# Differential attention: values as the stationary operand, column-tiled softmax sums, products in PSUM between groups, finalization on token tiles moved by transfers

## Chip, cores, metric

The kernel runs on the 8 cores of one Trainium2 chip. Each core takes half of one sequence of the batch (2048 of its 4096 tokens as queries, all 4096 as keys). The metric is device time of the slowest core in microseconds (us). A program on all 8 cores has a second, slower state in some executions (a die with a lower granted clock); only fast runs are compared here unless the text says otherwise.

Engines: PE is TensorE's matmul and PEld its weight load, DVE is VectorE, ACT is ScalarE, POOL is GpSimd, SP is SyncE, whose queue issues most transfers.

## The reference, cut to what matters

```python
h = rmsnorm(x); z = h @ w_in                    # q k v gate | B C h gate
s1 = q1 @ k1.T / sqrt(d) + bias                 # bias = -slope[h] * |t - s|, 4 heads, d = 64
s2 = q2 @ k2.T / sqrt(d) + bias
probs = softmax(s1) - lam * softmax(s2)
o = probs @ v                                   # v is 128 wide
o = rmsnorm(o) * subln_g * (1 - lambda_init) * silu(gate)
x = x + concat(o, conv_branch) @ w_out          # then a gated embedding and a final norm
```

The slopes are 1/4, 1/16, 1/64 and 1/256. Blocks so far from the diagonal that the exponential is zero are skipped, so head 0 has few tiles (10 or 13 a unit), head 1 has 19 to 31, and heads 2 and 3 have 35. A *unit* is one head and 512 queries; there are 16. A *tile* is 128 keys by up to 512 queries, for both score sets: a *full tile* has all 512.

## The kernel before

Attention works tile by tile, two tiles deep: score pair of tile i on PE, exponential on ACT, then PV of tile i-2 on PE. Keys above the diagonal (group B) and the rest (group AC) are accumulated apart, because the bias is split into a part per key (in the exponential's bias) and a part per query, which differs between the groups.

```python
# PV: the exponentials are stationary, the values (with a column of ones, so 129) move
for r in [j_*4 + b_ for j_ in range(2) for b_ in range(b0, b1)]:          # up to 8 matmuls
    PE.matmul(acc_region(r), lhsT=ET[e][:, j*512 + sb_*128 : ...+128], rhs=VA[:, kt, h, :], ...)
# group B's end: DVE copies three PSUM banks to SBUF times fB[query] (a query is a partition)
# group AC's end: DVE adds three PSUM banks to that; then the finalization:
DVE: reciprocal [128x8]; x neglam; 4 x scale; 4 x combine; square; reduce     # query on partitions
POOL: variance, pow(-1/2) [128x4], scale [128x512]
PE (12 tiles later): 4 transposes;  DVE: x subln x gate -> MIXA
```

Each engine runs its own program in order. `X.need(t)` puts a wait for event t into X's program; `pending` delays the emission of a piece of work by so many tiles. `barrier()` after the last unit separates attention from the output stage. Before it, PE has other work: the first output tile and 32 transposes.

Of the kernel before, what the change touches and what calls it, by code (L numbers as in the profile page):

```python
# [6 lines left out]
F32 = mybir.dt.float32  # L7
# [9 lines left out]
NH = 4  # L17
# [44 lines left out]
def build_program(debug=None):  # L62
# [25 lines left out]
    with es:  # L88
# [17 lines left out]
        VAF = sb("VA", [128, 32 * NH * 129], BF16)  # L106
# [29 lines left out]
        iotaF = sb("iotaF", [128, 4], F32)  # L136
        iotaB0 = sb("iotaB0", [128, 32], F32)
        iotaF0 = sb("iotaF0", [128, 2, 2], F32)
        biasA = sb("biasA", [128, NH, 16], F32)
        biasB = sb("biasB", [128, NH, 32], F32)  # L140
        fB = sb("fB", [128, NH, 8], F32)
        rs = [sb("rs%d" % i, [128, 8], F32) for i in range(2)]
        c2 = [sb("c2_%d" % i, [128, 4], F32) for i in range(2)]
        ssq = [sb("ssq%d" % i, [128, 4], F32) for i in range(2)]
        vsq = [sb("vsq%d" % i, [128, 4], F32) for i in range(2)]
        rsd = [sb("rsd%d" % i, [128, 4], F32) for i in range(2)]
# [35 lines left out]
        POOL.eng.memset(mx_all[:], 0.0)  # L182
        tk_pc = POOL.mark(POOL.eng.memset(VA[:, :, :, 128:129], 1.0))
# [3 lines left out]
        LC = {}  # L187

        def late_consts():
# [18 lines left out]
            POOL.eng.iota(iotaB0[:], pattern=[[128, 32]], base=-255, channel_multiplier=1, allow_small_or_imprecise_dtypes=True)  # L208
            POOL.eng.iota(iotaF0[:], pattern=[[0, 2], [256, 2]], base=-255, channel_multiplier=2, allow_small_or_imprecise_dtypes=True)
            t_io = POOL.mark(POOL.eng.iota(iotaF[:], pattern=[[256, 4]], base=-511, channel_multiplier=2,  # L210
# [3 lines left out]
            for h in range(NH):  # L214
                src_f = iotaF0[:].rearrange("p a b -> p (a b)") if h == 0 else iotaF[:]
                for j_ in range(2):
                    LC["t_f"] = ACT.mark(ACT.eng.activation(out=fB[:, h, 4 * j_:4 * j_ + 4], in_=src_f, func=AF.Exp, scale=SLOPES[h]))

# [23 lines left out]
        with pes:  # L242
# [154 lines left out]
            def v_tile(buf, tl, rglob, ready_tk):  # L397
                s = psp_next()
                PE.need(psP_free[s], w_ready[buf], ready_tk)
                ins = None  # L400
                for c in range(8):
                    ins = PE.eng.matmul(psP[s][:], lhsT=HT[:, c, tl * 128:(tl + 1) * 128], rhs=WB[buf][:, c, :],  # L402
                                        start=(c == 0), stop=(c == 7))
                tk = PE.mark(ins)
                flush_deferred()
                DVE.need(tk, tk_pc)
                psP_free[s] = DVE.mark(DVE.eng.tensor_copy(out=VA[:, rglob, :, 0:128],
                                                           in_=psP[s][:].rearrange("p (h d) -> p h d", h=NH)))
# [165 lines left out]
        OACC = [cv.take([128, 8, 129], F32) for _ in range(2)]  # L574
        OT = [cv.take([128, 4, 128], F32) for _ in range(2)]
        ON = [cv.take([128, 4, 128], F32) for _ in range(2)]
# [23 lines left out]
        rc2 = RawCarver(VAF[:], 32 * NH * 129 * 2)  # L600
# [52 lines left out]
        with pes:  # L653
            psS = [es.enter_context(nc.psum_tensor("psS%d" % i, [128, 1024], F32)) for i in range(2)]
            psBig = es.enter_context(nc.psum_tensor("psBig", [128, 2048], F32))
            psA = [psBig[:, b_ * 512:(b_ + 1) * 512] for b_ in range(3)]
            psO = psBig[:, 1536:2048]

            def acc_region(r):
                return psA[r // 3][:, (r % 3) * 129:(r % 3) * 129 + 129]  # L660
# [11 lines left out]
            for h in range(NH):  # L672
                for qc in range(4):
                    unit = h * 4 + qc
                    rel = range(-4 * qc, 32 - 4 * qc)
                    up = [(n, live_range(h, n, 0, min(n, 4))) for n in rel if n > 0]
                    past = [(n, live_range(h, n, 0, 4)) for n in rel if n < 0]
                    past = [e_ for e_ in past if e_[1]]
                    diag = [(n, (n, min(4, live_range(h, n, 0, 4)[1]))) for n in range(4)]
                    ac = past[:2]  # L680
                    rest = past[2:]
                    for d_ in diag:
                        ac.append(d_)
                        ac += rest[:1]
                        rest = rest[1:]
                    groups = [("B", up), ("AC", ac + rest)]
                    groups = [(g, [e_ for e_ in els if e_[1]]) for g, els in groups]
                    for gi, (g, els) in enumerate(groups):
                        last_mm = {}
                        for ki, (n, (b0, b1)) in enumerate(els):  # L690
                            for r in [j_ * 4 + b_ for j_ in range(2) for b_ in range(b0, b1)]:
                                last_mm[r // 3] = (ki, r)
                        for ki, (n, (b0, b1)) in enumerate(els):
                            tiles.append(dict(h=h, qc=qc, unit=unit, g=g, n=n, kt=4 * qc + n, b0=b0, b1=b1, ki=ki, last_mm=last_mm,
                                              first=(ki == 0), last=(ki == len(els) - 1),
                                              unit_last=(gi == len(groups) - 1 and ki == len(els) - 1)))
# [6 lines left out]
            acc_done = {}  # L703
            started = set()
            oacc_free = [None, None]
            ot_free = [None, None]
            on_free = [None, None]
            pso_free = [P1END["psM"]]
            pending = []
            unit_evac = {}  # L710
# [30 lines left out]
            def finalize_part1(unit, h, qc, tks):  # L741
                u = unit % 2
                DVE.need(tks, ot_free[u])
                t_ = DVE.mark(DVE.eng.reciprocal(out=rs[u][:], in_=OACC[u][:, :, 128]))
                DVE.need(t_, LC["tk_const"])
                t_c2 = DVE.mark(DVE.eng.tensor_scalar(out=c2[u][:], in0=rs[u][:, 4:8], scalar1=neglam[:], scalar2=None, op0=ALU.mult))
                DVE.need(t_c2)
                for sb_ in range(4):
                    t_ = DVE.mark(DVE.eng.tensor_scalar(out=OT[u][:, sb_, :], in0=OACC[u][:, 4 + sb_, 0:128],
                                                        scalar1=c2[u][:, sb_:sb_ + 1], scalar2=None, op0=ALU.mult))  # L750
                DVE.need(t_)
                for sb_ in range(4):
                    t_ = DVE.mark(DVE.eng.scalar_tensor_tensor(out=OT[u][:, sb_, :], in0=OACC[u][:, sb_, 0:128],
                                                               scalar=rs[u][:, sb_:sb_ + 1], in1=OT[u][:, sb_, :],
                                                               op0=ALU.mult, op1=ALU.add))
                oacc_free[u] = t_
                DVE.need(t_)
                DVE.need(on_free[u])
                t_ = DVE.mark(DVE.eng.tensor_tensor(out=ON[u][:], in0=OT[u][:], in1=OT[u][:], op=ALU.mult))
                DVE.need(t_)  # L760
                t_ = DVE.mark(DVE.eng.tensor_reduce(out=ssq[u][:], in_=ON[u][:], axis=AX.X, op=ALU.add))  # L761
                DVE.need(t_)
                POOL.need(t_)
                t_v = POOL.mark(POOL.eng.tensor_scalar(out=vsq[u][:], in0=ssq[u][:], scalar1=1.0 / 128.0, scalar2=EPS,  # L764
                                                       op0=ALU.mult, op1=ALU.add))
                POOL.need(t_v)
                t_p = POOL.mark(POOL.eng.tensor_tensor(out=rsd[u][:], in0=vsq[u][:], in1=mhalf[:].to_broadcast([128, 4]), op=ALU.pow))
                POOL.need(t_p, on_free[u])
                t_on = POOL.mark(POOL.eng.tensor_tensor(out=ON[u][:], in0=OT[u][:],
                                                        in1=rsd[u][:].unsqueeze(2).to_broadcast([128, 4, 128]), op=ALU.mult))  # L770
                ot_free[u] = t_on

                def part2():
                    PE.need(t_on, pso_free[0])
                    ins = None
                    for sb_ in range(4):
                        ins = PE.eng.transpose(out=psO[:, sb_ * 128:(sb_ + 1) * 128], in_=ON[u][:, sb_, :], identity=ident_f[:])  # L777
                    t_tr = PE.mark(ins)
                    on_free[u] = t_tr
                    DVE.need(t_tr)  # L780
                    t_m = DVE.mark(DVE.eng.scalar_tensor_tensor(out=MIXA[:, h, qc * 512:(qc + 1) * 512], in0=psO[:], scalar=sublns[:],  # L781
                                                                in1=SGA[:, h, qc * 512:(qc + 1) * 512], op0=ALU.mult, op1=ALU.mult))
                    pso_free[0] = t_m
# [310 lines left out]
```

## Time and profile before

| | before |
|---|---|
| median | 963.2 us (fast runs 961.1 to 963.3) |
| projections and convolution | to 366 us |
| attention, heads 0 and 1 | 149.5 us |
| attention, heads 2 and 3 | 279.7 us |
| hand-over (last PV to first output-stage addition) | 14.7 us |
| output stage | the rest |

The head of the page of the kernel before: span and the busy time of each engine, with its share.

```profile
span 961.9 us, 17031 instructions; the slowest of 8 cores (956.1 to 961.9 us)
...
PE 838.9 (87%) x6210; PEld 445.6 (46%) x6210; DVE 450.7 (47%) x814; ACT 584.3 (61%) x783; POOL 123.5 (13%) x155
```

Busy time by stretch, kernel before: rows are heads 0 and 1, heads 2 and 3, hand-over. After the busy times come the granted PE clock, the share of DMA and GB/s.

```profile
core 5: us, PE busy (x) PEld busy (x) DVE busy (x) ACT busy (x) POOL busy (x), PEclk, DMA share, GB/s
366.50:516.00 149.50, 126.41 (x1181) 74.60 (x1179) 69.03 (x174) 125.00 (x167) 20.61 (x27) 0.88 0.23 33
516.00:795.70 279.70, 255.02 (x2634) 154.15 (x2635) 70.29 (x183) 265.97 (x278) 17.91 (x24) 0.99 0.06 17
795.70:810.35 14.65, 9.75 (x52) 6.81 (x50) 5.93 (x17) 4.10 (x4) 2.24 (x3) 0.78 0.00 1
```

ACT is busy 266 of the 280 us of heads 2 and 3: that stretch is bound by the exponentials, and PE has room. Over the whole span PE has the largest share (87%), which says nothing of this stretch. The timeline of two full tiles of head 2 (start, length, engine, what):

```profile
599.74 7.15 ACT L737 ACTIVATE ARENA<-psS,biasB 128x1024 bf16<-128x1024 f32 x7
...
600.00 0.37 PE L718 MATMUL psS<-QT,KT 64*128 64x512 bf16 x1
...
600.00 0.39 PE L720 MATMUL psS<-QT,KT 64*128 64x512 bf16 x1
...
600.32 0.63 PE L805 MATMUL psBig<-VA,ARENA 128*128 128x129 bf16 x8
...
601.00 0.37 PE L718 MATMUL psS<-QT,KT 64*128 64x512 bf16 x1
```

A tile repeats every 1.007 us (600.00 to 601.00 and so on). ACT runs seven exponentials without a gap. PE is done at 600.95 and starts the next score pair when ACT frees the score buffer. The two score matmuls lie in the two row halves of the array and run together.

### The profile page before, as it was taken

How to read it: one execution, taken by the hardware profiler on the slowest of the kernel's cores; microseconds unless marked ns; L12 is line 12 of the kernel's file. 1: busy time of each engine (PE TensorE's matmuls, PEld its weight loads, DVE VectorE, ACT ScalarE, POOL GpSimd, SP SyncE). 2: the span in 40 equal slices, each digit the busy share in tenths (PEclk: the TensorE clock that was granted, in tenths of full speed). 3: DMA queues.
4: the chain of work that ended last, by engine and by line, in shares of the span. 5: the costliest groups of instructions: out<-in, count | busy, mean ns of one | idle time of the engine just before them, and what ended most of it. 6: DMA issues, size and time to landing. Idle time of an engine off the chain costs nothing.

```text
span 961.9 us, 17031 instructions; the slowest of 8 cores (956.1 to 961.9 us)
## 1 busy us (share of the span) xinstructions
PE 838.9 (87%) x6210; PEld 445.6 (46%) x6210; DVE 450.7 (47%) x814; ACT 584.3 (61%) x783; POOL 123.5 (13%) x155
## 2 busy tenths in 40 slices
PE   0688979999999996889889999899999897999993
PEld 0344434444444443445555555555555554444441
DVE  1577684343277667644432213312312313577775
ACT  2344554502211116779999999999999992455553
POOL 2221130011110002010000000000000001122222
PEclk9999999999999997888999999999999997999997
DMA  8763422055550006700000000000500000133332
GB/s 175 203 154 96 140 73 42 4 44 45 44 44 1 2 1 84 114 1 1 2 2 1 2 2 1 2 1 4 174 1 1 2 1 22 53 124 132 132 110 88
DMA packets 37920, 51.04 MB, mean 53 GB/s; under 512 B 18512, under 2 KB 29392, under 8 KB 37840
## 3 DMA queue, kind: packets, MB, share of 16 engines
q1 hardware_dynamic: 12336, 36.85, 12.0%
q0 software_dynamic: 25504, 13.11, 11.9%
q8 instruction: 52, 0.85, 0.4%
q14 instruction: 28, 0.23, 0.1%
HBM read 54.67 MB, written 8.39 MB: 66 GB/s over the span
## 4 chain that ended last, share of the span: by engine, by line
PE 61%; DVE 13%; ACT 12%; issue 8%; DMA 2%; POOL 2%; DVEq 0%; SPq 0%; ACTq 0%; POOLq 0%
PE psP L357 20%; PE psBig L805 16%; PE psS L718 11%; ACT ARENA L737 8%; PE psP L402 6%; DMA ARENA<-x 2%; PE psS L900 2%; PE psS L950 2%; POOL r L916 2%; DVE VA L961 2%; DVE VA L965 1%; DVE KT L904 1%; ACT SGA L911 1%; DVE psS L728 1%; PE psT L329 1%
## 5 line engine op out<-in xcount | busy, mean ns | idle before, releaser
L737 ACT ACTIVATE ARENA<-psS,biasB 128x1024 bf16<-128x1024 f32 (+3 forms) x292 | 264.2, 1007 | 14.7 <-PE psS L720 13.4
L805 PE MATMUL psBig<-VA,ARENA 128*128 128x129 bf16 x2904 | 254.7, 227 | 16.8 <-DVE ARENA L825 5.8
L357 PE MATMUL psP<-ARENA 128*128 128x512 bf16 x1024 | 232.3, 382 | 0.9 <-DVE ARENA L522 0.7
L805 PEld LDWEIGHTS psBig<-VA,ARENA 128*128 128x128 bf16 x2904 | 173.2, 100 | 110.0 <-issue 101.4
L718 PE MATMUL psS<-QT,KT 64*128 64x512 bf16 (+3 forms) x429 | 152.4, 355 | 35.3 <-ACT ARENA L737 23.7
L720 PE MATMUL psS<-QT,KT 64*128 64x512 bf16 (+3 forms) x429 | 156.4, 365 | 0.0
L357 PEld LDWEIGHTS psP<-ARENA 128*128 128x128 bf16 x1024 | 99.2, 98 | 117.1 <-issue 6.3
L737 ACT ACTIVATE ARENA<-psS,biasA 128x1024 bf16<-128x1024 f32 (+3 forms) x156 | 131.2, 896 | 25.8 <-DVE psS L728 18.1
L718 PEld LDWEIGHTS psS<-QT,KT 64*128 64x128 bf16 x429 | 39.9, 93 | 96.0 <-issue 84.6
L728 DVE SCALAR_TENSOR_TENSOR psS<-T_relu,psS 128x256 f32<-128x256 f32 x64 | 27.4, 427 | 90.9 <-PE psS L720 90.8
L329 PE MATMUL psT<-ident_b,ARENA 128*128 128x128 bf16 x256 | 22.2, 238 | 43.4 <-DVE ARENA L317 21.0
L950 PE MATMUL psS<-ARENA,QT 128*128 128x512 bf16 x256 | 58.4, 381 | 0.0
L402 PE MATMUL psP<-ARENA 128*128 128x512 bf16 x256 | 58.0, 379 | 0.0
L375 DVE TENSOR_REDUCE mx_all<-psM 128x1 f32<-128x512 f32 x48 | 33.1, 690 | 52.4 <-PE psM L372 51.0
L820 DVE TENSOR_TENSOR ARENA<-psBig,fB 128x387 f32<-128x387 f32 (+1 forms) x48 | 22.0, 509 | 67.8 <-PE psBig L805 67.1
L764 POOL TENSOR_SCALAR vsq<-ssq 128x4 f32<-128x4 f32 x16 | 3.1, 192 | 388.7 <-DVE ssq L761 388.7
L384 ACT ACTIVATE KT<-psP 128x512 bf16<-128x512 f32 x32 | 19.1, 596 | 52.0 <-PE psP L357 52.0
L781 DVE SCALAR_TENSOR_TENSOR ARENA<-psBig,sublns,SGA 128x512 bf16<-128x512 f32 x16 | 12.0, 751 | 81.1 <-PE psBig L777 81.1
L309 POOL TENSOR_TENSOR rstd_all<-v_all,mhalf 128x1 f32<-128x1 f32 x32 | 30.8, 964 | 105.5 <-DVE v_all L306 105.4
L825 DVE TENSOR_TENSOR ARENA<-psBig,ARENA 128x387 f32<-128x387 f32 (+1 forms) x48 | 22.3, 510 | 46.8 <-PE psBig L805 46.0
L329 PEld LDWEIGHTS psT<-ident_b,ARENA 128*128 128x128 bf16 x256 | 17.8, 106 | 52.2 <-issue 49.9
L302 ACT ACTIVATE ARENA<-ARENA 128x1024 bf16<-128x1024 f32 x32 | 33.8, 1057 | 10.8 <-DMA ARENA<-x 10.5
(111 smaller groups left out, 875.2 us busy)
## 6 DMA issues: line engine op xcount, KB each, us to landing
ARENA<-x SPq DMA_DIRECT2D x32, 512.0 KB, 3.8
KT<-x SPq DMA_DIRECT2D x16, 512.0 KB, 4.2
y<-VA SPq DMA_DIRECT2D x16, 512.0 KB, 2.9
ARENA<-w_in POOLq DMA_DIRECT2D x4, 1024.0 KB, 17.1
ARENA<-w_in POOLq DMA_DIRECT2D x16, 256.0 KB, 9.1
ARENA<-w_out POOLq DMA_DIRECT2D x2, 1024.0 KB, 13.1
ARENA<-w_g POOLq DMA_DIRECT2D x2, 1024.0 KB, 24.6
KT<-p SPq DMA_DIRECT2D x4, 512.0 KB, 12.4
```

What stands on the lines that cost most here:

```text
L302: tk_sq[i] = ACT.mark(ACT.eng.activation(out=JUNK[:], in_=XT[s][:], func=AF.Square, accum_out=ss_all[:, k:k + 1]))
L309: tk_r[i] = POOL.mark(POOL.eng.tensor_tensor(out=rstd_all[:, k:k + 1], in0=v_all[:, k:k + 1], in1=mhalf[:], op=ALU.pow))
L329: ins = PE.eng.transpose(out=psT[s2][:, c * 128:(c + 1) * 128], in_=XN[s2][:, c * 128:(c + 1) * 128], identity=ident_b[:])
L357: ins = PE.eng.matmul(psP[s][:], lhsT=WB[buf][:, c, wcol0:wcol0 + 128], rhs=HT[:, c, tokc * 512:(tokc + 1) * 512], start=(c == 0), stop=(c ...
L375: t_r = DVE.mark(DVE.eng.tensor_reduce(out=mx_all[:, idx:idx + 1], in_=psM[:], axis=AX.X, op=ALU.max))
L402: ins = PE.eng.matmul(psP[s][:], lhsT=HT[:, c, tl * 128:(tl + 1) * 128], rhs=WB[buf][:, c, :], start=(c == 0), stop=(c == 7))
L718: PE.eng.matmul(psS[b][:, x0:x1], lhsT=KT[0:64, h, kt * 128:(kt + 1) * 128], rhs=QT[0:64, h, qc * 512 + x0:qc * 512 + x1], start=True, sto ...
L720: tk_s = PE.mark(PE.eng.matmul(psS[b][:, 512 + x0:512 + x1], lhsT=KT[64:128, h, kt * 128:(kt + 1) * 128], rhs=QT[64:128, h, qc * 512 + x0: ...
L728: tk_in = DVE.mark(DVE.eng.scalar_tensor_tensor(out=dgb, in0=T_relu[:].unsqueeze(1).to_broadcast([128, 2, 128]), scalar=-2.0 * SLOPES[h], ...
L737: ins = ACT.eng.activation(out=ET[e][:].rearrange("p (j q) -> p j q", j=2)[:, :, s0 * 128:s1 * 128], in_=ps3[:, :, s0 * 128:s1 * 128], fun ...
L805: ins = PE.eng.matmul(acc_region(r), lhsT=ET[e][:, j * 512 + sb_ * 128: j * 512 + (sb_ + 1) * 128], rhs=VA[:, kt, h, :], start=st_, stop=f ...
L950: ins = PE.eng.matmul(psG[:, half_ * 512:(half_ + 1) * 512], lhsT=X1NT[s][:, c, :], rhs=WG[:, c, half_ * 512:(half_ + 1) * 512], start=(c ...
```

## The change

It is meant to take load off PE: eight PV matmuls with eight weight loads become two of 512 columns with the values stationary. The output then has queries along the free axis, so sums cannot ride along as a 129th column; they are made by matmuls with ones in four 32-column tiles of the array. The per-query factor between the groups is applied in place in PSUM. Reciprocals and powers are not computed on the replicated rows: the rows are taken through a scratch tensor in HBM to a compact tile [128 x 8] and back as a broadcast. Units of heads 1 and 0 alternate.

```diff
-for r in [...]:  PE.matmul(acc_region(r), lhsT=ET[e][: , 128 queries], rhs=VA[:, kt, h, 0:129])
+for j in range(2):
+    PE.matmul(psA[j][:, x0:x1], lhsT=VA[:, kt, h, :], rhs=ET[e][:, j*512+x0 : j*512+x1], start=unit_first)
+for q_ in range(4):                                   # four column tiles
+    PE.matmul(psL[32*q_:32*q_+32, a_:b_], lhsT=ones_b[:, 0:32], rhs=ET[e][...], start=q_ not in started)
 # between the groups
-DVE: OACC = psA * fB (three banks), later OACC += psA
+DVE: psA[0] *= FQ;  psA[1] *= FQ;  psL[0:64] *= FQ[..];  psL[64:128] *= FQ[..]     # in place; PE waits
 # finalization of a unit
+DVE: copy psL, psA[0], psA[1] to SBUF
+SP:  4 row writes -> scr1;  read scr1 -> L8 [128 x 8]
+part_a (5 tiles later):  DVE reciprocal L8;  SP write -> scr1b;  SP broadcast scr1b -> RB;  POOL 2 products
+part_b (7 later):        DVE combine;  POOL square
+part_c (3 later):        PE sums over partitions;  DVE variance;  SP 4 row writes;  read -> V4;
+                         POOL pow;  SP write;  SP broadcast -> RSB;  POOL product
+part_e (13 later):       DVE x subln x gate -> MIXA
...
+order = [u_ for q_ in range(4) for u_ in ((1, q_), (0, q_))] + [(h_, q_) for h_ in (2, 3) for q_ in range(4)]
```

## The prediction

> **What bounds the kernel now.** The profiled core spans 961.9 us: projections to about 366, attention 366 to 796, a 15 us hand-over, the output stage from 810. Only attention and hand-over change. In the timeline of head 2 a full tile repeats every 1.007 us, which is ScalarE's exponential back to back; TensorE uses about 0.95 of it (score pair about 0.33, eight PV matmuls 0.63 with their lead-in) and waits. By stretch, ScalarE is busy 129.1 of 135 us (520 to 655) and 133.5 of 141 (655 to 796). So heads 2 and 3 (280 us, 260 of them exponentials by start-to-start times) are bound by ScalarE; at most 20 us can go. Heads 0 and 1 take 150 us for 115 us of exponentials: there VectorE is busy 37 of 61 us, the mean granted clock is 0.77, and the waits are diagonal fixes (L728), evacuations and finalization queued in order on VectorE.
>
> **What changes, costed.** The exponentials stay, so TensorE relief in heads 2 and 3 buys nothing. In TensorE-bound places of the trace, eight 128-column steps cost 57 ns each, and each change between score pair and PV costs a further 0.11 us that halving the clock does not change. Estimate from these: PV becomes two 512-column matmuls, 0.43+0.11; the sums are four 256-column matmuls in separate column tiles. The Trainium skill, "TensorE: Matmul & The Clock Gate", Part 3, says such tiles run concurrently, about 4 ns apart; the score pair (10 ns apart) agrees for row tiles, no column tile is in this trace. "TensorEngine Tiling (Array Packing)", Key Properties, says a mode switch drains the array. So sums 0.12 plus 0.05 to 0.11. Total 0.33+0.54+0.2 = about 1.05 us a full tile against 1.007: TensorE becomes the limit, or nearly. Serial sums: near 1.4.
>
> Boundaries: between groups TensorE now waits for in-place PSUM products, 2x128x512 and 2x64x256 (estimated 2.0 us from the 128x387 evacuations at 0.45 start to start; before 1.35, released by bank). At a unit's end 0.3+0.6+0.6. Score buffers hide about 1.5 us of each. I expect about 1 us more a unit, +12 in all.
>
> Finalization frees VectorE (about 7.3 to 5.5 us a unit) but becomes eight dependent transfer steps of about 2 us (1.6 us for 4 KB and 2.9 to 3.8 for 512 KB in the transfer table) with POOL products of 1.04 us: about 29 us. In mid-attention the deferral by 5, 7, 3, 13 tiles roughly covers it, with stalls of TensorE or VectorE of 1 to 5 us while the output weights load (first units). After the last PV nothing covers it: 15 us becomes about 29.
>
> **Sum.** Tiles of heads 2 and 3: +10. Boundaries: +12. Last finalization: +14. Early stalls: +3. Heads 0 and 1, less VectorE queueing and a warmer clock through interleaving: -15. Net +24, about 987 us; 80% range 945 to 1030. Chances: faster 0.15, within 2% 0.33, slower 0.52.
>
> **What would show it.** The full-tile period near 1.05 with ScalarE waiting for the score matmul; the four sum matmuls starting within about 15 ns; ScalarE still about 390 us; VectorE PSUM products on the chain at group ends; last PV to first output-stage add about 29 us, of which most is transfers.
>
> **What would make it wrong.** Sums serialised (far slower); no drain between PV and sums, so ScalarE stays the limit and interleaving wins 20 us or more (faster); transfers far quicker or slower than 2 us, so the deferrals stall TensorE in every unit.

## The result

| | before | after |
|---|---|---|
| median | 963.2 us | 1145.0 us |
| fast runs | 961.1 to 963.3 | 1135.4 to 1145.5 |

The ratio is 1.186 (95% interval 1.179 to 1.194). It is the mean time of one kernel's fast runs over that of the other's of the same rounds, so not quite the ratio of the medians. The change is slower by 18.6%; the prediction had 987 us with a range to 1030.

The same views of the kernel after. First the page's head:

```profile
span 1134.3 us, 16262 instructions; the slowest of 8 cores (1104.2 to 1134.3 us)
...
PE 945.0 (83%) x5768; PEld 357.8 (32%) x5768; DVE 423.8 (37%) x686; ACT 604.8 (53%) x779; POOL 182.8 (16%) x189
```

PE has fewer instructions and is busy longer. The stretches, in the same order:

```profile
core 3: us, PE busy (x) PEld busy (x) DVE busy (x) ACT busy (x) POOL busy (x), PEclk, DMA share, GB/s
366.50:588.99 222.49, 174.30 (x1118) 50.51 (x1116) 53.84 (x113) 127.15 (x165) 43.95 (x40) 0.71 0.28 46
588.99:952.97 363.98, 314.37 (x2246) 91.64 (x2245) 59.58 (x123) 283.09 (x281) 49.83 (x44) 0.91 0.16 31
952.97:985.70 32.73, 8.90 (x56) 5.72 (x53) 3.61 (x7) 4.10 (x4) 5.79 (x5) 0.65 0.12 25
```

The three stretches add 73.0, 84.3 and 18.1 us, 175 in all; the rest of the kernel is 3 us shorter, which makes the 172.4 us between the two profiled spans. The clock fell from 0.88 to 0.71 and from 0.99 to 0.91.

These rows are of core 3, the slowest, and the second one is not typical. Cores 2 and 3 took 362 and 364 us for heads 2 and 3, the other six 343 to 345 (in the kernel before, all eight took 280 to 281). The cause of that difference stays open, but it goes with slower transfers: the 51 reads, write-backs and broadcasts of the finalizations in this stretch add to 173 and 176 us, from issue to landing, on cores 2 and 3 and to 130 to 136 on the others. In every fast run of the kernel after one pair of neighbouring cores, not always the same pair, is 14 to 25 us behind the middle of the eight. So a difference of the slowest cores mixes what the program costs with this, and the table of the experiments also gives the middle (median) of the eight cores.

Full tiles of head 2 in the timeline of PE:

```profile
700.02 0.29 PE L851 MATMUL psBig<-ARENA,ones_b 128*32 128x256 bf16 x4
700.25 0.39 PE L718 MATMUL psS<-QT,KT 64*128 64x512 bf16 x1
700.25 0.39 PE L720 MATMUL psS<-QT,KT 64*128 64x512 bf16 x1
700.57 0.61 PE L842 MATMUL psBig<-ARENA,VA 128*128 128x512 bf16 x2
701.11 0.29 PE L851 MATMUL psBig<-ARENA,ones_b 128*32 128x256 bf16 x4
701.33 0.39 PE L718 MATMUL psS<-QT,KT 64*128 64x512 bf16 x1
```

A tile now takes 1.083 us (700.25 to 701.33) with PE going from piece to piece: 0.32 to PV, 0.54 to the sums, 0.22 to the next pair. Four sum matmuls together take 0.29 us, and one alone takes 0.30 on average, so they do run side by side. The new tile costs what the prediction said it would (1.05), but 0.076 us times the 232 full tiles of heads 2 and 3 is 18 us, not 175.

The longest thing that is new is the finalization. At the end of attention one unit's chain runs with little in its way. This is the chain of work that ended last in the kernel after, in order of time (start, length, what), from the copy of the sums to the last product:

```profile
952.97 0.44 DVE ARENA L758
...
954.51 1.26 DMA scr<-ARENA
...
955.83 3.20 DMA ARENA<-scr
...
959.39 1.59 DMA scr1b<-ARENA
...
961.05 4.01 DMA ARENA<-scr1b
...
965.32 1.26 POOL ARENA L779
966.58 1.23 POOL ARENA L780
...
967.92 0.76 DVE ARENA L786
...
968.87 1.05 POOL ARENA L789
...
970.06 0.69 PE psBig L795 x8
...
972.32 1.24 DMA scr<-ARENA
...
973.63 2.78 DMA ARENA<-scr
...
976.54 1.02 POOL ARENA L810
...
977.64 1.43 DMA scr2b<-ARENA
...
979.15 4.15 DMA ARENA<-scr2b
...
983.43 1.26 POOL ARENA L819
...
984.79 0.76 DVE ARENA L825
```

It takes 32.6 us (952.97 to 985.55); the eight transfers in it add to 19.7. The combination (L786) comes 15.0 us after the start and PE's sums (L795) 17.1 us after it. In the program they stand 11 and 14 tiles after the unit's end (the deferrals add to 12 and 15, but the count starts with the tile that ends the unit). That is 11.9 and 15.2 us for full tiles, and less for head 0's short ones. So DVE and PE can reach these waits too early, and then everything behind them in their programs stands. The view of waits of the kernel after, whole span (who waited for what: total us, times, longest):

```profile
DVE ARENA L786 <- POOL ARENA L780: 152.0, 13, 25.0
...
ACT ARENA L737 <- PE psS L720: 115.8, 114, 15.8
...
PE psBig L795 <- POOL ARENA L789: 49.2, 9, 15.0
```

DVE stands 152 us for the products of the first half. Not all of this costs time (DVE has nothing else to do in parts of a group), but PE stands 49 us for the squares, once for 15 us, and ACT once for 15.8 us for a score pair that PE could not start. Of PE's 49 us, 33 are before the squares of three units of head 0; the units of 35 tiles add 0 to 2.5 us each, the last one 5.

### The profile page after: what moved, and what is told of

Its sections match the earlier page's. It is cut to its first block, busy times and chain, and to the rows that moved or that the text cites. A ratio compares the mean times of both kernels' runs of the same rounds, so it can differ in the third digit from the quotient of the medians.

```text
span 1134.3 us, 16262 instructions; the slowest of 8 cores (1104.2 to 1134.3 us)
## 1 busy us (share of the span) xinstructions
PE 945.0 (83%) x5768; PEld 357.8 (32%) x5768; DVE 423.8 (37%) x686; ACT 604.8 (53%) x779; POOL 182.8 (16%) x189
## 4 chain that ended last, share of the span: by engine, by line
PE 58%; DMA 16%; DVE 10%; issue 5%; POOL 5%; ACT 3%; SPq 2%; DVEq 0%; POOLq 0%; ACTq 0%
PE psP L353 17%; PE psBig L842 13%; PE psS L718 7%; PE psBig L851 6%; PE psP L398 5%; PE psS L934 3%; DMA ARENA<-scr1b 3%; PE psS L984 3%; DMA scr1b<-ARENA 3%; DMA ARENA<-scr 3%; DMA scr<-ARENA 2%; DMA ARENA<-x 2%; DMA ARENA<-scr2b 2%; SPq L57 2%; DMA scr2b<-ARENA 1%
## 5 line engine op out<-in xcount | busy, mean ns | idle before, releaser
L737 ACT ACTIVATE ARENA<-psS,biasB 128x1024 bf16<-128x1024 f32 (+3 forms) x292 | 281.1, 985 | 82.8 <-PE psS L720 81.4
L842 PE MATMUL psBig<-ARENA,VA 128*128 128x512 bf16 (+3 forms) x858 | 265.1, 390 | 35.7 <-DVE ARENA L760 16.0
L718 PE MATMUL psS<-QT,KT 64*128 64x512 bf16 (+3 forms) x429 | 168.3, 392 | 16.3 <-ACT ARENA L737 15.2
L720 PE MATMUL psS<-QT,KT 64*128 64x512 bf16 (+3 forms) x429 | 169.0, 394 | 0.0
L851 PE MATMUL psBig<-ARENA,ones_b 128*32 128x256 bf16 (+1 forms) x1540 | 132.6, 296 | 6.0 <-DVE psBig L866 6.0
L851 PEld LDWEIGHTS psBig<-ARENA,ones_b 128*32 128x32 bf16 x1540 | 44.5, 94 | 184.9 <-issue 181.9
L842 PEld LDWEIGHTS psBig<-ARENA,VA 128*128 128x128 bf16 x858 | 52.8, 100 | 142.3 <-issue 135.6
L786 DVE SCALAR_TENSOR_TENSOR ARENA<-ARENA,neglam 128x512 f32<-128x512 f32 x16 | 12.0, 751 | 152.0 <-POOL ARENA L780 152.0
L779 POOL TENSOR_TENSOR ARENA<-ARENA 128x512 f32<-128x512 f32 x16 | 20.2, 1264 | 281.8 <-DMA ARENA<-scr1b 264.7
L325 PE MATMUL psT<-ident_b,ARENA 128*128 128x128 bf16 x256 | 22.0, 236 | 40.6 <-DVE ARENA L313 19.9
L728 DVE SCALAR_TENSOR_TENSOR psS<-T_relu,psS 128x256 f32<-128x256 f32 x64 | 27.3, 429 | 73.1 <-PE psS L720 72.7
L795 PE MATMUL psBig<-ARENA,ones_f 128*32 128x128 f32 x128 | 8.8, 354 | 49.2 <-POOL ARENA L789 49.2
L863 DVE TENSOR_TENSOR psBig<-psBig,FQ 128x512 f32<-128x512 f32 x32 | 20.7, 694 | 66.8 <-PE psBig L851 66.8
```

What stands on the lines that cost most here:

```text
L718: PE.eng.matmul(psS[b][:, x0:x1], lhsT=KT[0:64, h, kt * 128:(kt + 1) * 128], rhs=QT[0:64, h, qc * 512 + x0:qc * 512 + x1], start=True, sto ...
L720: tk_s = PE.mark(PE.eng.matmul(psS[b][:, 512 + x0:512 + x1], lhsT=KT[64:128, h, kt * 128:(kt + 1) * 128], rhs=QT[64:128, h, qc * 512 + x0: ...
L728: tk_in = DVE.mark(DVE.eng.scalar_tensor_tensor(out=dgb, in0=T_relu[:].unsqueeze(1).to_broadcast([128, 2, 128]), scalar=-2.0 * SLOPES[h], ...
L737: ins = ACT.eng.activation(out=ET[e][:].rearrange("p (j q) -> p j q", j=2)[:, :, s0 * 128:s1 * 128], in_=ps3[:, :, s0 * 128:s1 * 128], fun ...
L842: PE.eng.matmul(psA[j][:, x0:x1], lhsT=VA[:, kt, h, :], rhs=ET[e][:, j * 512 + x0:j * 512 + x1], start=t["unit_first"], stop=t["unit_last" ...
L851: ins = PE.eng.matmul(psL[32 * q_:32 * q_ + 32, a_ - 256 * hf:b_ - 256 * hf], lhsT=ones_b[:, 0:32], rhs=ET[e][:, j * 512 + a_:j * 512 + b_ ...
```

## The experiments

Theory A: the chains of transfers cost the time. They are waited for in program order by DVE, PE and POOL, and PE's idling brings a lower clock. Theory B: the new tile and the boundaries are slower by themselves, and draw a lower clock, whatever the transfers do. Two side questions are whether the order of units helps or hurts, and why the kernel before spends 149.5 us on heads 0 and 1.

All of the following stretches are read from the profiled runs as above: from 366.5 us to DVE's copy at the end of the last unit of heads 0 and 1, from there to the copy of the last unit, from there to the output stage. The columns with times by stretch and clock are of the slowest core; the last two are the middle of the eight cores, read in the same way from each core's trace (in the kernel before, DVE's reciprocal stands for the copy). Runs with constants in place of transferred scales are wrong on purpose; their instruction counts and shapes are those of the real ones. "1 run" results are good for some 10 us.

| run | time | heads 0, 1 (clock) | heads 2, 3 (clock) | hand-over | middle core: heads 0, 1 | heads 2, 3 |
|---|---|---|---|---|---|---|
| before | 963 | 149.5 (0.88) | 279.7 (0.99) | 14.7 | 150.4 | 280.1 |
| after | 1145 | 222.5 (0.71) | 364.0 (0.91) | 32.7 | 222.5 | 344.0 |
| e3 no transfers | 1063 | 192.2 (0.75) | 334.6 (0.94) | 17.3 | 189.2 | 334.3 |
| e14 no first half's transfers | 1104 | 216.1 (0.72) | 342.3 (0.93) | 26.7 | 212.0 | 340.1 |
| e4 later emission | 1116 | 222.2 (0.72) | 344.6 (0.92) | 31.0 | 215.7 | 346.0 |
| e12 later emission and fill | 1133 | 229.9 (0.84) | 350.1 (0.96) | 34.8 | 227.6 | 338.8 |
| e13 second half from POOL's queue | 1175 | 238.3 (0.70) | 381.2 (0.90) | 37.8 | 240.9 | 361.8 |
| e5 = e3, no sums in heads 2, 3 | 1041 | 193.2 (0.75) | 313.4 (0.92) | 15.6 | 185.9 | 314.0 |
| e6 = e3, no products between groups | 1030 | 175.7 (0.80) | 320.3 (0.93) | 15.5 | 169.0 | 320.2 |
| e8 = e3, neither | 1006 | 176.2 (0.77) | 293.2 (0.95) | 15.5 | 172.9 | 292.7 |
| e7 = e3, PE filled at the pauses | 1031 | 172.4 (0.99) | 322.7 (1.00) | 16.7 | 171.2 | 322.7 |

### e3_no_transfers

```diff
-SP: 4 row writes, read -> L8      (and the write, the broadcast, and the second half's)
+L8, V4, RB, RSB: set to 1.0 once by POOL; POOL and DVE wait for the compute before them only
```

> The changed kernel with all eight transfer steps of each finalization taken out and its VectorE, POOL and TensorE work kept (scale tiles are constant ones, so the result is wrong on purpose). Theory A (latency of the transfer chains, waited for in program order by TensorE, VectorE, POOL and the DMA queue, and the low clock that TensorE's idling brings): attention falls from 587 to about 460 us (heads 0 and 1 from 222 to about 155, heads 2 and 3 from 364 to about 305), hand-over from 32 to about 17, granted clock back above 0.95, total 1000 to 1030. Theory B (the new tile itself is slower and draws a lower clock whatever the transfers do): total stays above 1090 and the clock near 0.90.

Measured: 1063 us (1 run). By stretch, the rows of the kernel without transfers:

```profile
366.50:558.69 192.19, 169.47 (x1127) 50.78 (x1127) 56.44 (x118) 128.42 (x167) 46.16 (x46) 0.75 0.18 26
558.69:893.32 334.63, 309.23 (x2246) 91.17 (x2245) 58.99 (x122) 282.47 (x281) 49.43 (x43) 0.94 0.05 14
```

Of the slowest cores, the transfers cost 30.3 + 29.4 + 15.5 = 75 us in the three stretches. On the middle core they cost 33 us in heads 0 and 1 and 10 in heads 2 and 3, and 8 of these 10 lie in the first unit of head 2, where the last finalization of head 0 still stands: the other seven units take 293 us with transfers (292 to 294 on six cores, 303 and 305 on cores 2 and 3) and 292 without. So the transfers are a large part, but 100 us of the loss are still there without a single one, and the clock is hardly better. Neither theory's forecast was met: each holds in part. The expectation of 155 us for heads 0 and 1 was far off.

In the timeline of PE in this run, the rows after one unit's end show what happens to the clock (start, length; in brackets PE's idle time before the row and what ended it):

```profile
602.43 0.22 PE L826 MATMUL psBig<-ARENA,VA 128*128 128x128 bf16 x1 [1.15 <-DVE ARENA L761]
603.03 0.22 PE L826 MATMUL psBig<-ARENA,VA 128*128 128x128 bf16 x1 [0.38 <-DVE ARENA L770]
...
606.21 1.03 PE L826 MATMUL psBig<-ARENA,VA 128*128 128x512 bf16 x2
...
607.97 0.60 PE L826 MATMUL psBig<-ARENA,VA 128*128 128x512 bf16 x2
```

PE stands 1.5 us for DVE's copies; about four us later the same two PV matmuls take 1.03 us instead of 0.60 (the granted clock is 0.55 from 606 to 608 us). The pause is paid twice, once standing and once at about half speed.

### e4_later

```diff
-defer(7, part_b); defer(3, part_c); defer(13, part_e)
+defer(12, part_b); defer(4, part_c); defer(10, part_e)
```

> The changed kernel with the second part of the finalization emitted 17 instead of 12 tiles after the unit's end, the third 21 instead of 15, the last 31 instead of 28. Nothing else changes. If only the place of the waits in each engine's order matters (the waits come a few us too early), total falls by 40 us or more, to below 1100. If the chain of one unit is simply longer than the unit (rival: throughput of the chains on one queue), little changes: above 1120.

Measured: 1116 us, correct (1 run). That is 20 to 30 us less than after's fast runs, short of the 40 foreseen. On the slowest cores nearly all of it seems to lie in heads 2 and 3 (364.0 to 344.6), but that is the pair of cores with slow transfers, which e4's run does not have: its eight cores take 344 to 347 us there, as six of after's do. On the middle core heads 0 and 1 gain 7 us (222.5 to 215.7), the first unit of head 2 gains 5 and the other seven lose 7. In the trace of the slowest core PE now stands 1.6 us for the squares of those three units of head 0, where it stood 33, but other waits have come: DVE waits 12.1 us for the sums of the third unit, where it waited 3.1. So moving the waits by five tiles moves the stalls more than it removes them.

### e2_headmajor

```diff
-order = [(1,0), (0,0), (1,1), (0,1), ...] + heads 2, 3
+order = head 0, head 1, head 2, head 3
```

> The changed kernel with the old order of units (head 0 first, then 1, 2, 3). If interleaving of long and short units is a help, as the prediction assumed, heads 0 and 1 get slower than 222 us: four head-0 units of 10 to 13 tiles follow each other, each shorter than a chain of some 30 us, so 120 us for head 0 and about 120 for head 1: total 1145 to 1165. If interleaving is what hurts, total falls below 1110.

Measured: 1156 us in the fast state, correct (a second run, 1168, was slow), in the range foreseen. That is 11 to 21 us above after's fast runs, so interleaving helps the changed kernel; it is not what hurts.

### e1_order_only

The same edit the other way: the kernel before, with the interleaved order.

> The kernel before with one part of the change alone: the order of units of heads 1 and 0 interleaved. The prediction credited interleaving with 15 us in heads 0 and 1 (150 us). If that is right: 945 to 955 us. If head 0's loss is inside its own units (finalization work on VectorE in front of diagonal fixes) and does not depend on its neighbours: within 5 us of before.

Measured: 968.1 us, ratio 1.004 (1.0001 to 1.0075), 3 rounds. In the kernel before, the order is worth nothing. The 15 us that the prediction credited to heads 0 and 1 rested on it, in part.

### e5_no_sums, e6_no_rescale, e8_both

All three on top of e3.

```diff
 e5: -for q_ in range(4):   (four sum matmuls a tile)
     +for q_ in range(4) if h < 2 or t["first"] or t["last"] else ():
 e6: -DVE: psA[0] *= FQ; psA[1] *= FQ; psL *= FQ (2)      (and PE's wait for them)
 e8: both
```

> On top of the run without transfers (1063 us, result wrong on purpose): in heads 2 and 3 the column sums are left out for all tiles but the first and last of a group. There a full tile took 1.083 us, of which I read 0.22 from the first sum matmul to the next score pair. If TensorE is the limit, the tile falls back to ScalarE's 1.007 and no further: about 210 full tiles x 0.076 = 16 us, plus 5 us from partial tiles; heads 2 and 3 from 335 to about 312, total about 1040. If something else than TensorE's work sets 1.083 (access to PSUM, the clock), nothing changes.

> On top of the run without transfers: the four in-place products between the groups are left out and TensorE doesn't wait there (wrong on purpose). In the trace TensorE stands 1.3 us and ScalarE up to 3.1 us at each such place, and the clock halves for 2 to 3 us after some of them. If these pauses matter through the clock too: 16 x 2.5 = 40 us less, about 1023. If only the pause itself: 16 x 1.3 = 21 us less, about 1042.

> On top of the run without transfers: no sums in heads 2 and 3 and no products between groups, so what is left of the change is PV with values stationary and the copies at a unit's end. If the pieces add: heads 2 and 3 near 290 us (before: 280), total about 1000 to 1010, the rest being heads 0 and 1. If less than 975, the new PV alone would be no loss.

Measured: 1041, 1030 and 1006 us (1 run each). The sums cost 21.2 us in heads 2 and 3 (334.6 to 313.4), as foreseen. The products cost 14.3 there and 16.5 in heads 0 and 1; e6 took 33 us off the total where the pauses alone would give 21 and pauses with the clock 40, so it lies between its two forecasts. Together they take 41.4 us off heads 2 and 3, a little more than 21.2 + 14.3. What is left there, 293.2 against 279.7, is the new PV with the copies at a unit's end and the finalization's compute. So the new PV alone is no gain either: in full tiles of e8 ACT sets the pace (16 exponentials without a gap in 16.19 us).

### e7_fill

On top of e3: before PE waits for DVE at a group's or unit's end it runs 4, 2 and 2 matmuls of 384 columns into an unused part of PSUM.

```diff
+if t["first"]: fill(4)        # then wait for psA[0]; fill(2); psA[1]; fill(2); psL
 PE.need(acc_free[j])
```

> On top of the run without transfers: TensorE fills its pauses at the group and unit ends with matmuls into an unused piece of PSUM (8 of 384 columns, about 1.3 us in all), so that the pause stays but TensorE is not idle. If the low clock (0.73 in heads 0 and 1, 0.92 to 0.96 in heads 2 and 3) comes from these pauses, it rises above 0.9 and total falls by 20 to 40 us. If the low clock comes from the short matmuls of heads 0 and 1 or from power, the clock stays and total is unchanged or some us longer.

Measured: 1031 us (1 run), 32 us less for more work. The rows of heads 0 and 1 and of heads 2 and 3:

```profile
366.50:538.86 172.36, 159.92 (x1249) 56.82 (x1249) 57.17 (x119) 125.50 (x166) 45.47 (x45) 0.99 0.20 29
538.86:861.55 322.69, 314.64 (x2374) 98.87 (x2373) 59.00 (x122) 279.39 (x281) 50.25 (x45) 1.00 0.05 14
```

The clock goes from 0.75 to 0.99 and from 0.94 to 1.00. So the low clock without transfers comes from PE's short pauses, not from PE's load, which the fill adds to, and not from short matmuls, which are all still there. The Trainium skill, "TensorE: Matmul & The Clock Gate", Part 1, describes this gate: activity in a window of about 3.4 us decides between full and half clock. That activity decides agrees with the numbers just given; the length of the window no run here shows.

### e12_after_fill, e15_fill_away

The correct kernel of e4 with the same fill; e15 leaves the fill out where a finalization's third part was emitted shortly before.

> The changed kernel, correct, with the later emission of the second run (1116 us) and the filler matmuls at group and unit ends. If the two repairs add as in the runs without transfers (32 us): about 1085, clock 0.94 or more. It would still lose to the kernel before by 10% or more, because the chains of transfers and the longer tile stay.

> As the run with later emission and fill (1133 us; without fill 1116), correct, but the fill is left out where a finalization's third part was emitted less than 7 tiles before, so TensorE does not wait on VectorE's read for the sake of the fill. If that wait undid the fill's gain: total below 1105, clock above 0.93. If pauses from transfers, not those at the boundaries, set the clock in the full kernel: about 1110 to 1130.

Measured: e12 1133 us (1 run), correct, 17 us more than e4 without fill. The clock did rise (0.72 to 0.84, 0.92 to 0.96), the time of the slowest core did not fall. I took this for PE's extra wait on DVE's read of the same bank, but the view of waits shows no such wait, in e12 or in e15, so that reason falls. e15 took 1133, 1139 and 1190 us, correct; all its runs count as slow.

Within e12's profiled run the cores differ by 46 us (1086 to 1132) though they run one program; in e4 by 11. The difference goes with the transfers again. In heads 2 and 3 the fill helps where they took as long as in e4 (there 128 to 136 us for the 51, and 344 to 347 us for the stretch): cores 0, 1 and 6 of e12 took 332 to 335 us with 131 to 132 us of transfers, and the four cores of e15's undisturbed die 335 to 338 with 131 to 138. On cores 4 and 5 of e12 the transfers took 173 and 164 us and the stretch 352 and 350. In heads 0 and 1 six of e12's cores had 130 to 139 us for 39 transfers, where e4's had 107 to 118, and took 224 to 230 us, against e4's 210 to 222; core 0, with 110 us, took 204. So the fill's gain is still there with the transfers in place, some 10 us in heads 2 and 3, and slow transfers take it away again on some cores. Why they are slow there, and whether the fill has a part in it, stays open.

### e13_pool_queue, e14_no_first_half

```diff
 e13: second half's six transfer steps:  -SP.need(..), dma(SP, ..)   +POOL.need(..), dma(POOL, ..)
 e14: first half's transfers taken out as in e3, second half's kept
```

> The changed kernel, correct, with the second half of each finalization (variance: four row writes, read, write, broadcast) issued from POOL's queue instead of SyncE's. Each chain stays as long or gets longer. If standing in each other's way on one queue is the cost: heads 0 and 1 fall from 222 to below 205 us, total below 1120. If the length of each chain is the cost: total 1130 to 1150.

> The changed kernel without the transfers of the first half (sums, reciprocals; wrong on purpose), the second half's kept. If two chains in each other's way are the cost, one half alone costs little: attention within 15 us of the run without any transfers, total 1070 to 1090 (the hand-over keeps some 8 us of transfers). If the length of waits is the cost, the second half keeps its share: 1095 to 1110.

Measured: e13 1175 us, correct (1 run); e14 1104 us (1 run). SP and POOL run their programs in order. Where a unit of head 0 follows one of head 1, the second half of the earlier finalization comes in them before the write-back, the broadcast and the products of the later one's first half. Rows from the timelines of DVE, SP and POOL in the kernel after, core 3, for the third and fourth unit (heads 1 and 0); the fourth unit ended at 459.69:

```profile
464.31 0.20 DVE L773 RECIPROCAL ARENA<-ARENA 128x8 f32<-128x8 f32 x1 [1.43 <-DMA ARENA<-scr]
...
468.33 0.35 SPq L57 DMA_DIRECT2D scr2b<-ARENA  x1
469.83 0.32 SPq L57 DMA_DIRECT2D ARENA<-scr2b  x1
470.24 0.39 SPq L57 DMA_DIRECT2D scr1b<-ARENA  x1
...
479.57 1.26 POOL L779 TENSOR_TENSOR ARENA<-ARENA 128x512 f32<-128x512 f32 x1 [4.49 <-DMA ARENA<-scr1b]
...
482.17 0.75 DVE L786 SCALAR_TENSOR_TENSOR ARENA<-ARENA,neglam 128x512 f32<-128x512 f32 x1 [17.65 <-POOL ARENA L780]
```

The fourth unit's reciprocals are ready at 464.5, but their write-back (scr1b) is issued at 470.24, behind the third unit's write and broadcast (scr2b). POOL's first product comes 19.9 us after the unit's end. In the next two units of head 0 it comes after 23.4 and 27.3 us (18 to 20 on three other cores looked at), in the units of 35 tiles after 12.1 to 15.0. Before the squares of these three units PE stands 7.1, 10.8 and 15.0 us.

Giving the second half a queue of its own made things worse, in every stretch. But e13 only moves the second half into POOL's program, where the next unit's products stand behind it (in the same two units the one ends at 501.2 and the other starts at 501.1; PE then stands 12.9, 6.8 and 12.2 us), and POOL also spends time on issuing (66 us busy in heads 0 and 1 where it was 44). In e14 the second half alone keeps most of the cost in heads 0 and 1 (216.1 of 222.5, with 192.2 for none) and less in heads 2 and 3 (342.3, with 334.6 for none). It too stands in the next unit's way: POOL starts the third unit's last product at 475.11 and the fourth unit's first one at 476.33, 18.5 us after that unit's end where it is 5.6 in e3, and PE stands 6.8, 7.0 and 3.4 us in the three units. So neither run acquits the order of the halves, and the traces show neighbouring units in each other's way in heads 0 and 1. No run frees the halves of each other, so what this order costs was not measured by itself.

### e9_before_pool, e10_before_fill, e11_before_pool_fill

Tries at a version that beats both, from the kernel before.

```diff
 e9:  -DVE: 4 scale, 4 combine, square          +POOL: 2 products [128x512] with broadcast, add, square
      (reduction on DVE 8 tiles later, transposes 5 after that)
 e10: +if h == 0: 2 filler matmuls of 256 columns before a tile's PV (4 at a group's start)
 e11: both
```

> The kernel before, with the finalization's scaling, combination and squares (13 of its VectorE operations, some 4 us a unit) moved to POOL as whole-tile products, and the rest deferred 8 and 13 tiles; no transfers, PV as before. If VectorE's queue is what costs heads 0 and 1 their time (as I predicted it would be for the change), 5 to 15 us less: 950 to 960. If not, within 3 us.

> The kernel before, with two filler matmuls of 256 columns in front of each PV group of head 0 (not just after the transposes), so that TensorE is not idle there. Clock in heads 0 and 1's first 55 us is 0.74 now. If the low clock costs time there: the clock rises above 0.9 and total falls by 4 to 10 us. If VectorE and ScalarE set the pace there: no gain, or a few us lost.

> Both of the two preceding edits on the kernel before. If VectorE's queue and the low clock are separate costs, the gains add: 940 to 955.

Measured, 3 rounds each, all correct: e9 960.8 us, ratio 0.996 (0.993 to 0.9996); e10 967.9, ratio 0.997 of fast runs (0.992 to 1.001; its median counts two slow runs in); e11 963.6, ratio 0.999 (0.996 to 1.003). In e10 the clock over the first 54 us of attention rose to 0.85 (0.74 before), in e9 DVE's work in the same stretch fell from about 34 to 25.5 us. Neither moved the time by half a per cent. So in the kernel before neither DVE's queue nor the clock is what holds head 0, and no version here beats it by anything that matters.

## Why the prediction was wrong, point by point

| term of the prediction | said | measured |
|---|---|---|
| full tile | 1.05 us | 1.083 us |
| tiles of heads 2 and 3 | +10 | +21 (sums, by e5) |
| boundaries, all units | +12 | +31 (products alone, by e6) |
| stalls by transfers in attention | +3 | +60 (30.3 + 29.4, by e3); +43 on the middle core (33 + 10) |
| last finalization | +14 | +18 (15 by e3) |
| heads 0 and 1, gain | -15 | no gain (e1, e9) |
| total | +24 | +182 (medians) |

The measured terms add to 130 us. Most of the rest is what e8 leaves without transfers, sums (in heads 2 and 3) and products: 26.7 us in heads 0 and 1 and 13.5 in heads 2 and 3 more than before, which the prediction did not foresee.

- *What bounds the kernel now*: right. Exponentials bind heads 2 and 3, and PE's relief bought nothing there; even with sums and products taken out (e8) that stretch did not get below before.
- *Cost of a tile*: right in kind and nearly in size. Of two things the prediction took from the Trainium skill, one held: column tiles run together ("TensorE: Matmul & The Clock Gate", Part 3; four in 0.29 us). The trace agrees with the other, that a change of array mode drains the array and so costs time ("TensorEngine Tiling (Array Packing)", Key Properties): at the 57 ns per 128 columns that the prediction read from before, with score pair and sums running together, the tile's columns need an estimated 14 x 57 ns = 0.80 us, and it took 1.083. No run isolates the changes of mode. What was mis-sized is what follows when PE becomes the limit: partial tiles pay too, so the sums cost 21 us, not 10.
- *Boundaries "+12 in all"*: too small by a factor of 2.6 for the products alone. The prediction counted the pause (2.0 us, of which 1.5 hidden). It left out that the pause also halves PE's clock for some us afterwards. e7 fills the pauses, adds work, and gains 32 us: that is about the price of the clock (it overlaps with the 31 us of e6 and does not add to it).
- *"The deferral by 5, 7, 3, 13 tiles roughly covers it, with stalls ... (first units)"*: this step failed, and of the terms it is the furthest off: +3 was said, and e3 puts the cost at 60 us on the slowest cores and 43 on the middle one. The chain's length was foreseen (29 us; 32.6 measured with little in its way), and in heads 2 and 3, with 35 tiles to a unit, the deferral did cover it on six of eight cores (293 us with transfers and 292 without, from the second unit of head 2 on). It failed in heads 0 and 1: a unit of head 0 ends 17.5 to 19.7 us after the one before it (copy to copy on core 3), while that unit's chain takes 32 us or more. There the finalizations of two units overlap in the in-order programs of SP and POOL, which the prediction did not consider. The first products came up to 27.3 us after a unit's end, and DVE and PE stood behind them; with transfers heads 0 and 1 took 33 us more than without, and the first unit of head 2 took 8 more (middle core). The size is measured by e3; that the overlap is its cause is read from the traces.
- *"Heads 0 and 1 ... -15"*: failed. Interleaving alone (e1) and a DVE with less to do (e9) are worth nothing in the kernel before, and the "warmer clock" turned into a colder one, 0.71.
- *Last PV to first addition "about 29 us, of which most is transfers"*: 32.7, of which 19.7 are transfers. Right in kind, 4 us short.
- *"Transfers far quicker or slower than 2 us, so the deferrals stall TensorE in every unit"* was named as what would make the prediction wrong. The stalls came, but with transfers of about the length foreseen (19.7 us for eight at the end, against eight times 2) where the halves of two units met.

What is not settled: without transfers and with a warm clock (e7), heads 0 and 1 still take 172 us, 23 more than before (171 and 150 on the middle cores). The tile of two blocks has one more array mode than before and PE is busy 160 of the 172 us, part of it filler, which points to the tile again; no run took that apart. Nor is it settled why transfers are slower on some cores of some runs, which costs the slowest core of the kernel after some 20 us in heads 2 and 3, or what the order of the halves costs by itself.

## What to carry to other kernels

Look for the engine that binds the stretch you change; taking work off another one gained nothing here (e8), and the relieved engine ended up as the limit. When work is deferred by a fixed number of tiles so that a chain has time to finish, take the chain's length at each wait against the shortest unit, and look at what the next unit has put behind it in the same in-order programs: here the units of 35 tiles lost next to nothing on six of eight cores, and heads 0 and 1 lost 33 us. Where PE must pause a microsecond or two, count the half clock after it as well as the pause; a few filler matmuls show in one run how much that is. And before a difference of two slowest cores is explained, read the same stretch on all eight: some 20 of the 84 us lost in heads 2 and 3 were lost on two cores only.

## What the Trainium skill lacked or had wrong

- "TensorE: Matmul & The Clock Gate", in its table of goals, warns of idle gaps above about 3 us; its section on PSUM-queue cycling says that short idle spells between groups of matmuls also make the clock swing, but gives no length for them. Here gaps of 1.15 and 0.38 us at a unit's end were followed by matmuls at about half speed (1.03 instead of 0.60 us for the same two), and filling such gaps raised the mean granted clock from 0.75 to 0.99.
- "TensorEngine Tiling (Array Packing)" says that a mode switch drains the array and gives no size for it. With three modes a tile (row tiles, whole array, column tiles) the steps were 0.32, 0.54 and 0.22 us, an estimated 0.28 us a tile more than its columns need at 57 ns per 128.
- "DMA: Bandwidth & Descriptors", Anatomy of one DMA, gives a fixed cost of about 2 us for the SWDGE path. No page has a chain of dependent transfers of a few KB through HBM scratch from SP's queue: the eight steps of a finalization took 1.2 to 4.2 us each, 19.7 us together, and the whole chain with its compute 32.6 us.
